# A two-layer decoder trunk on one core: the SwiGLU's second product in seven products of quarters, with two sums of weight quarters made by accumulating DMAs

## The chip, the cores and the metric

The kernel runs on one core of a Trainium2 chip. What is measured is the device time of one execution in microseconds (us). It is given as the median of several runs, and beside it stands one execution that the hardware profiler recorded, whose span is the time from the first instruction of the program to the last.

## The reference

528 tokens (16 learned meta tokens ahead of 512) of width 1024 go through two layers. Each layer is a half-step SwiGLU, a mixer (retention in layer 0, gated linear attention in layer 1) and another half-step SwiGLU, each behind an RMSNorm; a final RMSNorm follows and the meta tokens are dropped. All arrays are float32. The part that the change is about:

```python
def swiglu(x, w_in, w_out):
    gate, up = jnp.split(x @ w_in, 2, axis=-1)      # w_in [1024, 2 * 2816]
    return (jax.nn.silu(gate) * up) @ w_out          # w_out [2816, 1024]

for i in range(DEPTH):
    h = h + 0.5 * swiglu(rmsnorm(h, norm_ffn1[i]), ffn1_w_in[i], ffn1_w_out[i])
    h = h + mixer_i(rmsnorm(h, norm_mix[i]))
    h = h + 0.5 * swiglu(rmsnorm(h, norm_ffn2[i]), ffn2_w_in[i], ffn2_w_out[i])
```

## The kernel before

**Layout.** Activations lie with features on the 128 partitions and tokens along the free dimension: the residual stream is eight tiles of 128x528, the hidden layer of a SwiGLU 22 tiles. A weight chunk of 128x1024 holds, side by side, eight blocks of 128x128.

**Precision.** Every float32 operand is split into a high part (a cast, on ScalarE) and a low part (what is left, on VectorE). A product of 128x128 by 128 x tokens is three matmuls: high by high, high by low, low by high (`mm3`, lines 295 to 298). Each piece of 512 weight columns so costs one cast (`whi`, L119, ACT) and one subtraction (`wlo`, L120, DVE). DVE is VectorE, ACT ScalarE, PE TensorE, POOL GpSimd, SP SyncE.

**Weights.** The class `Weights` holds the whole plan of the weights in their order of use. It loads chunks on SP's queue into four buffers (`_load`, L88), makes pieces up to `AHEAD` = 4 ahead of the product that uses them (`fetch`, called by `hook` after each block of matmuls) and keeps seven pieces.

**Seven products of quarters.** A *unit* (`unit`) makes two tiles of a product by Winograd's form of Strassen's scheme. The weights of two tiles form a 2x2 matrix of quarters a11, a12, a21, a22 (each 128x512: half of a chunk, four blocks of 128x128), the activations one of b11 to b22 (four row tiles by half of the tokens). Seven products of quarters do the work of eight. A quarter takes 4 x 3 = 12 matmuls, a unit 84. The four sums of weight quarters s1 = a21 + a22, s2 = s1 - a11, s3 = a11 - a21 and s4 = a12 - s2 are made on DVE (`_piece`, L105); those of the activations, t1 to t4, once per sublayer (`t_sums`). A unit uses three single banks of PSUM, X, Y and Z; sums of them are taken out by DVE and ACT between the quarters, `with urgent()`, which puts these instructions ahead of others that are ready.

**A SwiGLU (`ffn`).** There are four: f1 and f2 of layers 0 and 1. The 22 hidden tiles come in six groups. The first group's four tiles are made by plain products (48 matmuls for each tile of gates and each of what they gate), while the norm, the sums t and the split of the normed input are made. The other 18 tiles are made in nine pairs, a unit for the gates (`g`) and one for what they gate (`u`). The second product of a group (`out_steps`) is plain: eight steps, one for each row tile d of the result, with (tiles of the group) x 2 halves of the tokens x 3 matmuls. These steps stand between the quarters of the next group's units; the last group's follow by themselves and feed the next sublayer (`feed`), which needs scaled and squared copies of each finished row tile. Matmuls are 264 columns wide; in the last SwiGLU, which drops the meta tokens, 256.

**Retention** uses the same units for 14 of its products; gated linear attention uses none. The row sums of the norms go through `pow` on POOL (L341, L414). In the kernel before, that is all that POOL does.

**Order.** Engines take their instructions in order. A scheduler lays this order out from the program's order and its priorities when the program is built, and may so place an instruction that is ready ahead of one that is not.

Of the kernel before, what the change touches and what calls it, by code (L numbers as in the profile page):

```python
# [16 lines left out]
P = 128  # L17
HP = P // 2
D = 1024
KD = D // P  # L20
NM = 16
# rows kept for the meta tokens
# [11 lines left out]
# keys by partitions: tiles, keys in each, and where a tile has its scores, of the queries from its own on  # L34
# [3 lines left out]
# tokens by partitions: first token, tokens in a tile, tiles; then the same of the tile that is left;  # L38
# and how many of their tokens are not in another tile
# [11 lines left out]
class Weights:  # L51
    """Streams weight chunks from DRAM and splits them, in pieces of 512 columns, into two float32r parts."""

    # the pieces of a unit: quarters of two chunks a1, a2 of 128 rows of the product, and their sums
    UNIT = ("a11", "s2", "s1", "s3", "a12", "s4", "a22")
    FIRST = ("s2", "s1", "a11", "s3", "a12", "s4", "a22")

    def __init__(self, tc, ctx, raw_bufs=4, bufs=7):
        self.nc = tc.nc
        self.raw_pool = ctx.enter_context(tc.tile_pool(name="wraw", bufs=raw_bufs))  # L60
        self.pool = ctx.enter_context(tc.tile_pool(name="wsplit", bufs=bufs))
        self.raw_bufs, self.bufs = raw_bufs, bufs
        self.chunks, self.raw = [], {}
        self.plan, self.parts, self.sums = [], {}, {}
        self.loaded = self.done = self.split = self.taken = 0
        self.live = set()
        self.sum_pool = None

    def add(self, key, ap):
        n = ap.shape[1]  # L70
        c = len(self.chunks)
        self.chunks.append(ap)
        for o in range(0, n, PW):
            self.plan.append((key, c, o, min(PW, n - o), o + PW >= n))

    def add_unit(self, key, ap1, ap2, order, between=lambda: None):
        c = len(self.chunks)
        self.chunks += [ap1, ap2]
        for q in order:
            if q == "s3":  # L80
                between()
            self.plan.append((key + (q,), c, q, PW, {"s4": c, "a22": c + 1}.get(q)))

    def _load(self):
        while self.loaded < min(self.done + self.raw_bufs, len(self.chunks)):
            ap = self.chunks[self.loaded]
            t = self.raw_pool.tile([P, CW], F32, tag="raw", name=f"raw{self.loaded}")
            self.nc.sync.dma_start(t[:, :ap.shape[1]], ap)  # L88
            self.raw[self.loaded] = t
            self.loaded += 1  # L90

    def _piece(self, c, q):
        """The column range q of a chunk, or a quarter or a sum of quarters of a pair of chunks."""
        V = self.nc.vector
        if not isinstance(q, str):
            return self.raw[c][:, q:q + PW]
        if q[0] == "a":
            o = (int(q[2]) - 1) * PW
            return self.raw[c + int(q[1]) - 1][:, o:o + PW]
        if (c, q) not in self.sums:  # L100
            a, b, op = {"s1": ("a21", "a22", V.tensor_add), "s2": ("s1", "a11", V.tensor_sub),
                        "s3": ("a11", "a21", V.tensor_sub), "s4": ("a12", "s2", V.tensor_sub)}[q]
            a, b = self._piece(c, a), self._piece(c, b)
            t = self.sum_pool.tile([P, PW], F32, tag="wsum", name=f"w{q}_{c}")
            op(t, a, b)  # L105
            self.sums[c, q] = t
        return self.sums[c, q]

    def _split(self, upto):
        oldest = min(self.live, default=self.taken)  # L110
        upto = min(upto, len(self.plan), oldest + self.bufs)
        while self.split < upto:
            i = self.split
            _, c, q, n, last = self.plan[i]
# [8 lines left out]
            if last not in (None, False):  # L123
                self.raw.pop(c if last is True else last)
                self.done += 1
                self._load()

    def prime(self, n=None):
        bufs = self.raw_bufs
        self.raw_bufs = n or bufs  # L130
        self._load()
        self.raw_bufs = bufs

    def get(self, key):
        """The pieces of a chunk, or a piece of a unit, that come next."""
# [24 lines left out]
def trunk(ctx, tc, a):  # L160
# [10 lines left out]
    # ---------------- plan of the weight chunks, in the order of use  # L171
    def plan_ffn(w_in, w_out, layer, which):
        def out(gi, ds):
            f0, f1 = GROUPS[gi]
            for d in ds:
                W.add((which, layer, "o", gi, d), w_out[layer, d, :, f0 * P:f1 * P])

        for gi, (f0, f1) in enumerate(GROUPS):
            if gi == 0:
                for f in range(f0, f1):  # L180
                    W.add((which, layer, "g", f), w_in[layer, f])
                    W.add((which, layer, "u", f), w_in[layer, NF + f])
                continue
            ds = list(range(KD))
            per = KD // (f1 - f0)
            for f in range(f0, f1, 2):
                for s, o in (("g", 0), ("u", NF)):
                    mine, ds = ds[:per], ds[per:]
                    W.add_unit((which, layer, s, f), w_in[layer, o + f], w_in[layer, o + f + 1],
                               W.FIRST if gi == 1 and f == f0 and s == "g" else W.UNIT,  # L190
                               lambda: out(gi - 1, mine[:per // 2]))
                    out(gi - 1, mine[per // 2:])
        out(len(GROUPS) - 1, range(KD))
# [5 lines left out]
    def plan_ret():  # L199
        for h in range(RH):  # L200
# [6 lines left out]
            for s, o in (("rv", 16), ("rg", 32)):  # L207
                for m in range(0, 4, 2):
                    c = o + 4 * h + m
                    if h == 0 and s == "rv":  # L210
                        W.add((s, h, m), a["ret_in"][c])
                        W.add((s, h, m + 1), a["ret_in"][c + 1])
                    else:
                        W.add_unit((s, h, m), a["ret_in"][c], a["ret_in"][c + 1],
                                   W.FIRST if h == 0 and m == 0 else W.UNIT)
# [28 lines left out]
    plan_ffn(a["f2_in"], a["f2_out"], 1, "f2")  # L244

    # ---------------- constants and the residual stream
# [17 lines left out]
    V.memset(half_neg, -0.5)  # L264

# [17 lines left out]
    def hook():  # L283
        """Between blocks of matmuls: what waits for its place in TensorE's order."""
# [15 lines left out]
    # Of PSUM, half is pairs of banks; the other half is single banks in a SwiGLU, elsewhere a pair and two banks.  # L300
# [16 lines left out]
    def proj(ps_out, w, off, nk, xh, xl, rng):  # L317
        """ps_out[m, t] = sum over nk row tiles of w's 128 columns times x."""
# [116 lines left out]
    def pair(t, halves):  # L435
        """[128, tokens] as the halves, which are equal"""
# [5 lines left out]
    def t_sums(pool, name, th, tl, halves, k, u1, u2):  # L442
# [4 lines left out]
        n = u1.shape[1]  # L447
        t = pool.tile([P, 4, n, 264], F32, tag="su", name=f"tt{name}{k}")[:, :, :, :wd]
        V.tensor_sub(t[:, 0], u1[:, :, b0:b1], u1[:, :, a0:a1])
        V.tensor_sub(t[:, 1], u2[:, :, b0:b1], t[:, 0])  # L450
        V.tensor_sub(t[:, 2], u2[:, :, b0:b1], u1[:, :, b0:b1])
        V.tensor_sub(t[:, 3], u2[:, :, a0:a1], t[:, 1])
        hi, lo = [o[k // 2][:, :, k % 2:k % 2 + n, :wd] for o in (th, tl)]
        for j in range(0, 4, 4 // n):
            c = slice(j, j + 4 // n)
            split(hi[:, c], lo[:, c], t[:, c])

    def unit(key, name, first, halves, th, tl, pool, mid, done):
# [1045 lines left out]
```

## Time and profile before

| | |
|---|---|
| median of three runs | 2157.18 us (2157.05 to 2157.83) |
| profiled execution: span | 2155.8 us |
| mean granted TensorE clock | 0.999 |
| SwiGLU f1 of layer 0: first matmul at | 6.24 us |
| retention: first matmul at | 372.11 us |
| SwiGLU f2 of layer 0 | 810.51 us |
| SwiGLU f1 of layer 1 | 1172.16 us |
| gated linear attention | 1533.81 us |
| SwiGLU f2 of layer 1 | 1794.27 us |

For the profiled execution the profiler gives the span alone; the median of the runs, which holds what lies around the span too, is 1.4 us longer. In the profile's lists a group of instructions stands as line, engine, operation, output <- inputs, shape and count; after the bar its busy time, the mean duration of one in ns, and the idle time of its engine just ahead of it with what ended it. Buffer numbers are left out, so `po_f` is the PSUM tile of the second product in all four SwiGLUs.

### The profile page before, as it was taken

To read this page: it belongs to the slowest core of one execution; us is meant where nothing else is said; L and a number is where in the kernel's file an instruction comes from. 1 tells how busy PE (TensorE), PEld (TensorE's weight loads), DVE (VectorE), ACT (ScalarE), POOL (GpSimd) and SP (SyncE) were. 2 spreads that over 40 slices of the span, in tenths; PEclk is the share of its full clock that TensorE was granted. 3 is DMA by queue.
4 is the path that set the end of the run, shared out by engine and by line. 5 is a ranking of instruction groups with operands and counts; after the bars stand their busy time and mean duration, and the time that the engine had idled before them with its cause. 6 is when DMAs were issued, how large, how long until landed. Compare 5 with 4: busy or idle time off the path is not lost.

```text
span 2155.8 us, 42829 instructions
## 1 busy us (share of the span) xinstructions
PE 2138.7 (99%) x17454; PEld 2121.4 (98%) x17454; DVE 1699.6 (79%) x3105; ACT 990.6 (46%) x1843; POOL 20.8 (1%) x25
## 2 busy tenths in 40 slices
PE   8999999999999999999999999999999999999998
PEld 8999999999999999999999999999999999999998
DVE  7887787977676788798787878787775659798886
ACT  5454445444444454454444444444633234454444
POOL 0000000000000000000000000000000000000000
PEclk9999999999999999999999999999999999999999
DMA  4333334232323222333333233333321122333332
GB/s 147 99 107 95 104 99 131 71 99 79 99 79 99 79 79 60 98 104 103 99 94 113 70 96 102 108 99 100 107 70 59 60 77 71 94 103 99 108 99 79
DMA packets 71844, 201.28 MB, mean 93 GB/s; under 512 B 8032, under 2 KB 13536, under 8 KB 71648
## 3 DMA queue, kind: packets, MB, share of 16 engines
q1 hardware_dynamic: 70640, 195.26, 29.8%
q10 hardware_dynamic: 1008, 3.29, 0.5%
q8 instruction: 137, 2.24, 0.4%
q14 instruction: 59, 0.48, 0.1%
HBM read 196.42 MB, written 2.10 MB: 92 GB/s over the span
## 4 chain that ended last, share of the span: by engine, by line
PE 97%; DVE 2%; ACT 1%; issue 0%; POOL 0%; DMA 0%; POOLq 0%; DVEq 0%; ACTq 0%
PE po_f L296 8%; PE po_f L297 8%; PE po_f L298 8%; PE po_r L298 1%; PE po_r L296 1%; PE po_r L297 1%; PE lv L1147 1%; PE po L296 1%; PE gv L296 1%; PE pk L296 1%; PE pk L297 1%; PE gv L298 1%; PE gv L297 1%; PE pk L298 1%; PE gg L296 1%; PE gg L298 1%
## 5 line engine op out<-in xcount | busy, mean ns | idle before, releaser
L119 ACT CAST whi<-raw 128x512 fp32r<-128x512 f32 (+1 forms) x653 | 397.2, 610 | 595.7 <-PE gv L297 50.0
L120 DVE TENSOR_TENSOR wlo<-raw,whi 128x512 fp32r<-128x512 f32 (+1 forms) x653 | 437.7, 673 | 94.4 <-ACT whi L119 89.5
L297 PE MATMUL po_f<-hlf,whi 128*128 128x264 f32 (+1 forms) x1344 | 380.8, 283 | 0.0
L296 PE MATMUL po_f<-hhf,whi 128*128 128x264 f32 (+1 forms) x1344 | 380.8, 283 | 0.0
L298 PE MATMUL po_f<-hhf,wlo 128*128 128x264 f32 (+1 forms) x1344 | 380.3, 283 | 0.0
L119 ACT CAST whi<-ws 128x512 fp32r<-128x512 f32 x344 | 213.1, 621 | 341.3 <-PE po_f L297 91.7
L120 DVE TENSOR_TENSOR wlo<-ws,whi 128x512 fp32r<-128x512 f32 x344 | 235.4, 685 | 23.5 <-ACT whi L119 21.4
L298 PEld LDWEIGHTS po_f<-hhf,wlo 128*128 128x128 f32 x1344 | 253.0, 188 | 0.0
L296 PEld LDWEIGHTS po_f<-hhf,whi 128*128 128x128 f32 x1344 | 253.0, 188 | 0.0
L297 PEld LDWEIGHTS po_f<-hlf,whi 128*128 128x128 f32 x1344 | 252.7, 188 | 0.0
L670 DVE SCALAR_TENSOR_TENSOR xa<-po_f,xa 128x528 f32<-128x528 f32 (+1 forms) x184 | 129.1, 701 | 109.4 <-PE po_f L298 108.7
L105 DVE TENSOR_TENSOR ws<-raw 128x512 f32<-128x512 f32 x86 | 59.3, 689 | 36.3 <-DMA raw<-in_f_in 36.2
L298 PE MATMUL po_r<-ogh,wlo 128*128 128x264 f32 x256 | 73.0, 285 | 0.0
L296 PE MATMUL po_r<-ogh,whi 128*128 128x264 f32 x256 | 72.9, 285 | 0.0
L297 PE MATMUL po_r<-ogl,whi 128*128 128x264 f32 x256 | 72.6, 284 | 0.0
L324 ACT CAST hhf<-uf 128x528 fp32r<-128x528 f32 (+1 forms) x88 | 55.3, 628 | 31.8 <-DVE uf L624 21.4
L325 DVE TENSOR_TENSOR hlf<-uf,hhf 128x528 fp32r<-128x528 f32 (+1 forms) x88 | 61.4, 699 | 3.9 <-ACT hhf L324 1.4
L105 DVE TENSOR_TENSOR ws<-ws,raw 128x512 f32<-128x512 f32 x86 | 59.0, 686 | 0.8
L105 DVE TENSOR_TENSOR ws<-raw,ws 128x512 f32<-128x512 f32 x86 | 58.8, 683 | 0.4
L105 DVE TENSOR_TENSOR ws<-raw,raw 128x512 f32<-128x512 f32 x86 | 58.7, 683 | 0.1
L296 PEld LDWEIGHTS po_r<-ogh,whi 128*128 128x128 f32 x256 | 48.3, 189 | 0.0
L297 PEld LDWEIGHTS po_r<-ogl,whi 128*128 128x128 f32 x256 | 48.3, 189 | 0.0
(647 smaller groups left out, 7065.0 us busy)
## 6 DMA issues: line engine op xcount, KB each, us to landing
raw<-in_f_in SPq DMA_DIRECT2D x176, 512.0 KB, 3.5
raw<-in_f_out SPq DMA_DIRECT2D x160, 256.0 KB, 2.7
raw<-in_ret_in SPq DMA_DIRECT2D x48, 512.0 KB, 3.5
raw<-in_gla_in SPq DMA_DIRECT2D x25, 512.0 KB, 3.5
raw<-in_ret_o SPq DMA_DIRECT2D x16, 512.0 KB, 3.5
raw<-in_f_out SPq DMA_DIRECT2D x32, 128.0 KB, 2.2
raw<-in_gla_o SPq DMA_DIRECT2D x8, 512.0 KB, 3.4
xa<-in_xT SPq DMA_DIRECT2D x8, 264.0 KB, 5.1
```

What stands on the lines that cost most here:

```text
L105: op(t, a, b)
L119: self.nc.scalar.copy(hi[:, :n], raw[:, :n])
L120: self.nc.vector.tensor_sub(lo[:, :n], raw[:, :n], hi[:, :n].bitcast(F32))
L296: nc.tensor.matmul(ps, lhsT=lh, rhs=rh, start=start, stop=False, **kw)
L297: nc.tensor.matmul(ps, lhsT=lh, rhs=rl, start=False, stop=False, **kw)
L298: nc.tensor.matmul(ps, lhsT=ll, rhs=rh, start=False, stop=stop, **kw)
L324: S.copy(hi, src)
L325: V.tensor_sub(lo, src, hi.bitcast(F32))
L670: ins = V.scalar_tensor_tensor(xv, ps[d][:, :, :wd], scale, xv, ALU.mult, ALU.add)
L1147: nc.tensor.matmul(ps[:, j, J * P:J * P + n], lhsT=Kt[:, j, J * P:(J + 1) * P], rhs=q, start=(J == 0), stop=(J == 3), skip_group_check=True)
```

## The change

The second product is made in units too. Two row tiles d, d + 1 of the result and a group of hidden tiles form the 2x2 matrix of weights, so the groups are now of eight, eight and six tiles (in the last SwiGLU six, six, six, and the last four tiles stay plain). With eight tiles a quarter has four blocks, with six three blocks (384 columns, 9 matmuls). A hidden pair of tiles is now kept as seven blocks of activations, high and low: its own three quarters and the four sums t (`hidden`, which calls `t_sums`). The first four tiles of the hidden layer stay plain products and join the first group.

A group's four units of the second product stand between the first `g` unit and the first `u` unit of the next group; the last group's come right behind its last `u` unit.

The signs move from the weights to the activations (n11, n21, n22 and n3 are negated) and to the taking out, so that the four sums become additions: s1 = a21 + a22, s3 = a21 + a11, s2 = s1 + a11, s4 = a12 + s2. Of the four sums of weights, s1 and s3 are made in a buffer `pair`, into which two plain loads on SP put a11 and a22, and a DMA from POOL's queue then adds a21 to both; s2 and s4 stay on DVE. Each unit, those of retention too, so loads the chunk a1 (`raw`), two quarters and an accumulating one into `pair`, and a quarter a22 (`half`). `pair` and `half` have two buffers each, `raw` three, pieces six.

In `unit`, the single bank X takes four of the seven products one after another, and a pair of banks QZ the other three; X is copied or read by ACT or DVE between them. The order of the pieces is now a11, s1, s2, a12, s3, s4, a22; in the first unit of a SwiGLU s1, s2, a11, a12, s3, s4, a22.

```diff
-GROUPS = ((0, 4), (4, 6), (6, 10), (10, 14), (14, 18), (18, 22))
+GROUPS = ((0, 8), (8, 16), (16, 22))
+LAST_GROUPS = ((0, 6), (6, 12), (12, 18), (18, 22))
+NPL = 4
...
-    UNIT = ("a11", "s2", "s1", "s3", "a12", "s4", "a22")
+    UNIT = ("a11", "s1", "s2", "a12", "s3", "s4", "a22")
+    FIRST = ("s1", "s2", "a11", "a12", "s3", "s4", "a22")
+    SUMS = {"s2": ("s1", "a11"), "s4": ("a12", "s2")}
...
+        n = self.width[c] = ap1.shape[1] // 2
+        self.loads["raw"].append((c, (ap1,)))
+        self.loads["pair"].append((c, (ap1[:, :n], ap2[:, n:], ap2[:, :n])))
+        self.loads["half"].append((c, (ap2[:, n:],)))
         for q in order:
+            self.plan.append((key + (q,), c, q, n, {"s3": ["pair"], "s4": ["raw"], "a22": ["half"]}.get(q, [])))
...
+                if kind == "pair":
+                    t = self.pair_pool.tile([P, 2, PW], F32, tag="pair", name=f"pair{c}")[:, :, :n]
+                    for i in range(2):
+                        nc.sync.dma_start(t[:, i], aps[i])
+                    nc.gpsimd.dma_start(t, aps[2].unsqueeze(1).broadcast_to([P, 2, n]), accum_op=ALU.add)
...
+    WITH = {"a11": ("n11", "X"), "s1": ("t1", "Z"), "s2": ("t2", "X"), "a12": ("n21", "Q"), "s3": ("n3", "X"),
+            "s4": ("n22", "Z"), "a22": ("t4", "X")}
...
+                if q == "s1":
+                    S.copy(su[:, 2], to["Z"])
+                elif q == "a11":
+                    S.copy(su[:, int(first)], X)
+                    if first:
+                        V.tensor_sub(su[:, 0], su[:, 1], su[:, 3])
+                elif q == "s2":
+                    S.copy(su[:, 3 if first else 1], X)
+                elif q == "s3":
+                    c22(X, su[:, 2])
+                elif q == "s4":
+                    row1(su[:, :2], QZ)
+                elif q == "a22":
+                    c21(X)
...
+            def hidden(f, y):
+                ...
+                    h = hp.tile([P, 2, 7, 264], F32R, tag="H", name=f"h{me}{f}")
+                    hi, lo = h[:, 0, :, :wd], h[:, 1, :, :wd]
+                    split(hi[:, 4], lo[:, 4], y[:, 0, a0:a1])
+                    t_sums(up_, f"{me}h{f}", halves, y[:, 0], y[:, 1], h[:, 0, :4], h[:, 1, :4])
+                    split(hi[:, 5:], lo[:, 5:], pair(y[:, 1], halves))
...
+            def unit_o(gi, d):
+                hs = H[gi]
+                ...
+                def row1(ab, qz):
+                    o = pair(x[d], halves)
+                    V.scalar_tensor_tensor(o, ab, -0.5, o, ALU.mult, ALU.add)
+                    ins = V.scalar_tensor_tensor(o, qz, -0.5, o, ALU.mult, ALU.add)
+                    if feed and gi == len(groups) - 1:
+                        feed(d, ins)
+
+                def c22(c, s):
+                    o = x[d + 1][:, b0:b1]
+                    V.scalar_tensor_tensor(o, s, 0.5, o, ALU.mult, ALU.add)
+                    V.scalar_tensor_tensor(o, c, 0.5, o, ALU.mult, ALU.add)
+
+                def c21(c):
+                    o = x[d + 1][:, a0:a1]
+                    ins = V.scalar_tensor_tensor(o, c, 0.5, o, ALU.mult, ALU.add)
+                    if feed and gi == len(groups) - 1:
+                        feed(d + 1, ins)
```

More of the change, by code (lines that the diff above doesn't have):

```diff
@@ new lines, in _piece @@
+        n = self.width[c]
+        if q in ("a11", "a12"):
+            o = n if q == "a12" else 0
+            return self.tiles["raw", c][:, o:o + n]
+        if q == "a22":
+            return self.tiles["half", c][:, :n]
+        if q in ("s1", "s3"):
+            return self.tiles["pair", c][:, int(q == "s1")]
+        if (c, q) not in self.sums:
+            a, b = [self._piece(c, i) for i in self.SUMS[q]]
+            t = self.sum_pool.tile([P, PW], F32, tag="wsum", name=f"w{q}_{c}")[:, :n]
+            self.nc.vector.tensor_add(t, a, b)
@@ L113, in _split @@
             i = self.split
-            _, c, q, n, last = self.plan[i]
+            _, c, q, n, over = self.plan[i]
             self._load()
@@ L122, in _split @@
             self.split += 1
-            if last not in (None, False):
-                self.raw.pop(c if last is True else last)
-                self.done += 1
+            for kind in over:
+                del self.tiles[kind, c]
+                self.over[kind] += 1
                 self._load()
     def prime(self, n=None):
-        bufs = self.raw_bufs
-        self.raw_bufs = n or bufs
+        room = self.room
+        if n:
+            self.room = {"raw": n, "half": 0, "pair": 0}
         self._load()
-        self.raw_bufs = bufs
+        self.room = room
     def get(self, key):
@@ L169, in trunk, with ffn_steps @@
     W = Weights(tc, ctx)
[L172 to L193, printed above, removed]
+    def ffn_steps(last):
+        steps = [("p", s, f) for f in range(NPL) for s in "gu"]
+        outs = []
+        groups = LAST_GROUPS if last else GROUPS
+        for gi, (f0, f1) in enumerate(groups):
+            for f in range(max(f0, NPL), f1, 2):
+                steps.append(("i", "g", f))
+                steps += outs
+                outs = []
+                steps.append(("i", "u", f))
+            plain = last and gi == len(groups) - 1
+            outs = [("l" if plain else "o", gi, d) for d in range(0, KD, 1 if plain else 2)]
+        return steps + outs
```

452 lines of the change are left out of this document (235 added, 217 removed).

## The prediction

> **What bounds the kernel now.** I read the page first, for the busy shares and the chain that ended last; then what TensorE waited for; then stretches of steady work.
>
> ```profile
> span 2155.8 us, 42829 instructions
> ...
> PE 2138.7 (99%) x17454; PEld 2121.4 (98%) x17454; DVE 1699.6 (79%) x3105; ACT 990.6 (46%) x1843; POOL 20.8 (1%) x25
> ...
> PE 97%; DVE 2%; ACT 1%; issue 0%; POOL 0%; DMA 0%; POOLq 0%; DVEq 0%; ACTq 0%
> ```
>
> ```profile
> PE pf10g L296 <- ACT whi L119: 6.2, 1, 6.2
> PE sc L296 <- DVE pl L325: 1.3, 4, 0.3
> ...
> PE bc_ro L349 <- DVE dg_ro L343: 0.7, 3, 0.3
> ```
>
> PE is busy all through, the chain is PE's own order for 97%, and its waits come to some 10 us in all, 6.2 of them the start. So matmuls taken out shorten the span one for one, as long as nothing else becomes late; and each new wait of PE costs its length. DVE, busy for 79%, is next.
>
> ```profile
> 950.00:1122.00 172.00, 172.00 (x1415) 172.00 (x1415) 140.58 (x255) 80.11 (x152) 0.00 (x0) 1.00 0.34 100
> 1860.00:2100.00 240.00, 240.00 (x2034) 240.00 (x2033) 199.97 (x366) 113.68 (x220) 0.00 (x0) 1.00 0.34 103
> 811.00:860.00 49.00, 49.00 (x399) 48.45 (x398) 42.72 (x69) 22.51 (x37) 1.53 (x2) 1.00 0.21 63
> ```
>
> These are stretches of two SwiGLUs (columns: length, then PE, PEld, DVE, ACT, POOL, then clock, DMA share and GB/s). One matmul of 264 columns takes 172.00 / 1415 = 0.1216 us, one of 256 columns 240.00 / 2034 = 0.1180. In the third, a SwiGLU's start with its plain products, DVE is busy for 87%.
>
> **What is removed.** The second product has 22 x 8 x 2 x 3 = 1056 matmuls in a SwiGLU; four times that, less the 192 of the last four tiles (`pl`), is 4032, and the page agrees (three groups of 1344):
>
> ```profile
> L297 PE MATMUL po_f<-hlf,whi 128*128 128x264 f32 (+1 forms) x1344 | 380.8, 283 | 0.0
> ```
>
> In units it is 11 pairs x 4 units x 7 x 3 = 924, so 132 fewer in three SwiGLUs; in the last, 18 tiles go from 864 to 756, 108 fewer. 396 x 0.1216 + 108 x 0.1180 = **60.9 us** less PE work. Units of the hidden layer and of retention keep their 84 matmuls.
>
> **What DVE gets.** Its costs by shape:
>
> ```profile
> L120 DVE TENSOR_TENSOR wlo<-raw,whi 128x512 fp32r<-128x512 f32 x621 | 424.4, 686 | 93.8 <-ACT whi L119 89.0
> L670 DVE SCALAR_TENSOR_TENSOR xa<-po_f,xa 128x528 f32<-128x528 f32 x144 | 101.5, 705 | 86.1 <-PE po_f L298 85.6
> L105 DVE TENSOR_TENSOR ws<-ws,raw 128x512 f32<-128x512 f32 x86 | 59.0, 686 | 0.8
> L624 DVE TENSOR_TENSOR uf<-uf,gf 128x264 f32<-128x264 f32 x81 | 34.0, 426 | 0.0
> L325 DVE TENSOR_TENSOR tlf<-ttf,thf 128x1056 fp32r<-128x1056 f32 x12 | 14.8, 1250 | 0.0
> L369 DVE SCALAR_TENSOR_TENSOR ula<-xa,gains,uha 128x528 fp32r<-128x528 f32 x40 | 30.3, 766 | 8.9 <-ACT uha L367 8.8
> L377 DVE TENSOR_TENSOR sqa_n<-sqa_n,sq_n 128x528 f32<-128x528 f32 x35 | 24.5, 701 | 0.1
> ```
>
> and two rows of its order of time:
>
> ```profile
> 2119.01 0.69 DVE L120 TENSOR_TENSOR wlo<-raw,whi 128x512 fp32r<-128x512 f32 x1
> ...
> 2119.61 0.42 DVE L624 TENSOR_TENSOR uf<-uf,gf 128x256 f32<-128x256 f32 x1
> ```
>
> They show that an instruction listed with 0.69 us lets the next start after 0.60; so sums of durations are an upper bound of DVE's time, and 0.60 / 0.69 = 0.87 of them a lower one. A hidden pair (units g and u, 168 matmuls, 20.4 us of PE) costs DVE after the change: 14 low parts and 4 sums of weights, 18 x 0.686 = 12.3; taking out, 3 of 528 and 4 of 264 columns, 3 x 0.70 + 4 x 0.43 = 3.8; `hidden`, 5 x 0.43 + 1.25 + 0.70 = 4.1. Together 20.2 us, by the lower bound 17.6. Before, four more sums (2.7) and more taking out stood against a `hidden` of 1.4. A unit of the second product (10.2 us of PE) costs 9 x 0.686 + 2 x 0.705 + 3 x 0.43 = 8.9 (lower 7.7); a plain step of four tiles cost 0.686 + 0.705 for 2.9 us of PE. A group of eight tiles, four pairs and four units, so loads DVE with 100 to 117 us per 122.5 us of PE, against 140.58 of 172 before. DVE stays below PE; I take no loss here, with a price in the first rival. At the start of a SwiGLU, `hidden` adds 2 x (4.1 - 1.4) = 5.4 to 42.72 of 49 us: full, not over.
>
> **Where PE will newly wait.** First, behind the last `u` unit. Before, steps of the group ahead stood there:
>
> ```profile
> 2119.57 0.28 PE L298 MATMUL Yf21u<-thf,wlo 128*128 128x256 f32 x1
> 2119.69 0.28 PE L296 MATMUL po_f<-hhf,whi 128*128 128x256 f32 x1
> ...
> 2122.51 0.28 PE L296 MATMUL pl<-hhf,whi 128*128 128x256 f32 x1
> ```
>
> That is 2.8 us of cover. Afterwards the last group's units follow at once and need the pair just made: c21 0.43, the sums t up to 4 x 0.43, a cast of 1056 columns about 1.1, its low part 1.25, so 3.2 to 4.5 us, over which PE has the products of the other two pairs, some 2 us. I take 2 us for each of the four SwiGLUs, **8 us** (ends 0 and 18).
>
> Second, bank X. In all orders but FIRST one quarter of another bank (1.46 us; 1.09 with three blocks) stands between two uses of X. What taking out needs:
>
> ```profile
> 510.87 0.29 PE L298 MATMUL Xrv<-uha,wlo 128*128 128x264 f32 x1
> ...
> 511.64 0.37 ACT L486 COPY surv<-Xrv 128x264 f32<-128x264 f32 x1
> ...
> 512.33 0.29 PE L298 MATMUL Yrv<-rth,wlo 128*128 128x264 f32 x1
> ...
> 512.73 0.43 DVE L490 TENSOR_TENSOR surv<-Yrv,surv 128x264 f32<-128x264 f32 x1 [0.27 <-PE Yrv L298]
> ```
>
> From the start of the last matmul ACT is done after 1.14 us and DVE after 0.83, so 1.0 and 0.7 past the time at which the next matmul could begin: below 1.46, and just below 1.09. In FIRST, a11 follows s2 in X with nothing between: 1.0 us in four SwiGLUs, **4 us** (0 to 4). For late turns in the 24 units of three blocks I take **3 us** (0 to 24, at 1 us each).
>
> Third, the last group with its feed: a unit of three blocks (63 x 0.1216 = 7.7 us of PE) costs DVE 9 x 0.55 (between 0.686 and the 0.43 of 264 columns) + 2.7 + two low parts and two sums of squares, 2 x (0.77 + 0.70): 10.6, lower 9.2. Four of them fall 6 to 12 us behind; pieces made ahead (2.4 us) and squares put off (4 x 1.4 = 5.6) cover the lower end. **3 us** for three SwiGLUs (ends 0 and 35).
>
> **The accumulating DMAs.** No row shows one. The nearest:
>
> ```profile
> raw<-in_f_in SPq DMA_DIRECT2D x176, 512.0 KB, 3.5
> raw<-in_f_out SPq DMA_DIRECT2D x160, 256.0 KB, 2.7
> ...
> q1 hardware_dynamic: 70640, 195.26, 29.8%
> ```
>
> ```profile
> L414 POOL TENSOR_TENSOR rc<-ms_n,half_neg 128x4 f32<-128x4 f32 (+2 forms) x11 | 9.1, 844 | 1177.1 <-DVE ms_n L412 1177.1
> ```
>
> 256 KB more take 0.8 us. The 512 KB of sums cost at least 3.5 us; if each byte costs like three plain ones (read, read, write), 2.7 + 5 x 0.8 = 6.7. I take the middle, 5.1. With 2.7 to 3.5 for the two loads ahead, which POOL has to wait for, the chain is 6 to 10 us. Its cover: a buffer's reload starts once s3 of its unit is split, and s1 of the unit after next is needed 10.5 pieces later, 10.5 x 1.46 = 15.3 us, 11.5 with three blocks. So it is hidden, at **0**. What hides it is PE's own work; each us beyond would cost half a us per unit (two buffers), 134 units. Traffic rises from 100 GB/s at a share of 0.34 to 1.84 MB per 10.2 us = 180 GB/s, a share of about 0.6, or 0.8 if the second read counts; landings get longer, but the engines are not full. The Trainium skill (Collectives: The Full Stack, "The bandwidth ceiling: the fold count and why AG ≠ RS ≠ AR") says that an add inside the DMA engine costs no time of its own but needs two source reads on one ring, half the rate of a copy. By that rule the sum is the 5.1 taken above; no row here can show it.
>
> On POOL, `pow` (0.84 us) queues behind a DMA that waits for its loads, and PE's broadcast of the norm for `pow`: at most 3.5 us at each of the norms that fall among units, five of them; the loads are long there by then in most, so 0 (up to 17). SP issues four loads for a unit in place of two, in the order in which buffers come free. I cost them at nothing: the transfers have the same 15 us.
>
> **Sum.** 2155.8 - 60.9 + 8 + 4 + 3 + 3 = 2112.9 us of span; with the 1.4 us by which the median stands above the span, **2114 us**.
>
> **Rivals.** *DVE becomes the bound.* If its instructions cost their full durations, the last groups cost 35 us in place of 3: 2146. For it: 20.2 us per 20.4 of PE leaves nothing to catch up with. Against: the rows above start after 0.60. *Turns of X are late all through.* Three turns in 134 units at 0.1 us are 40 us: 2154, no change. For it: DVE is fuller, and takes its order as laid out. Against: today's rows, 0.6 us to spare. *The sums land late, and the kernel is slower.* The place is ACT's cast of s1, behind which its copies out of X queue. It decides from a chain of 15.3 us, and eats the whole gain at 15.3 + 43 / 67 = 15.9; at 17 us it costs 1.7 x 67 = 114: 2228. For it: twice the traffic, POOL's descriptors and queue, none of it in the trace. Against: it needs an accumulation of 12 us, over three times a plain load. The Trainium skill (SBUF — State Buffer, "Who interferes with whom") says that a DVE instruction in a two-port mode keeps POOL from writing descriptors, while one with two SBUF inputs only blocks POOL's reads. By the first each accumulation could start later by one DVE instruction, 0.7 us, and stay inside the cover; no row here can show which holds. That the change doesn't do what it says can't be as to the matmuls, which are counted.
>
> **How the numbers follow.** Forecast 0.64 (2096 to 2134), DVE 0.14, turns 0.08, late sums 0.14. A measurement of this kernel tells 0.2% (4.3 us) from no change. The first counts as faster; DVE is split 0.07, 0.04, 0.03 and turns 0.05, 0.02, 0.01 (faster, same, slower); late sums are slower. That is 0.76, 0.06, 0.18. The range is 2096, all waits at nothing, to 2160, past the first two rivals.
>
> **What would show it.** Right: `po_f` units gone from plain steps, PE near 16950 instructions, its idle time under 35 us and at the ends of SwiGLUs; DVE at 85% or more. DVE's bound shows as waits of PE for `wlo`, the turns as waits of X's matmuls for c22 or copies, late sums as ACT's `whi` waiting for a DMA into `pair`. Wrong would be steady waits in mid-SwiGLU.

## The result and the profile after

The changed kernel takes **2473.14 us** (median; 2470.57 to 2474.71), against 2157.14 us (2157.05 to 2157.83) for the kernel before on the same chip: a ratio of 1.146, with a 95% interval of 1.145 to 1.148. Forecast were 2114 us and a range to 2160. It is slower by 316 us, and 359 us away from the forecast.

The page of the changed kernel, its span, busy time and DMA queues:

```profile
span 2468.4 us, 43589 instructions
...
PE 2208.8 (89%) x16950; PEld 2164.6 (88%) x16950; DVE 1746.6 (71%) x3183; ACT 1154.2 (47%) x2220; POOL 184.8 (7%) x159
...
q1 hardware_dynamic: 96560, 228.83, 29.2%
q0 software_dynamic: 36448, 67.12, 17.2%
```

The matmuls went as counted: 17454 - 16950 = 504. But PE now stands idle for 2468.4 - 2208.8 = 259.6 us, where it was 17.1, and its busy time has grown by 70.1 us although 60.9 us of work are gone. So 242.5 us are waits and 131 us (70.1 + 60.9) are matmuls at a slower pace. The records of the granted clock bear this out: it was 0.50 for 272 us, and half of that is 136 us. No engine is full, and DVE's share fell to 71%, which points to latency rather than throughput.

What PE waited for (total, times, longest):

```profile
PE Xf11o L339 <- DVE xa L698: 27.6, 7, 8.7
PE Xf10o L339 <- DVE xa L698: 26.6, 7, 7.4
PE Xf20o L339 <- DVE xa L698: 24.9, 7, 7.1
PE Xf21u L339 <- DVE yf L672: 20.3, 6, 4.6
...
PE Xf11g L339 <- ACT suf11g L525: 13.2, 4, 3.6
```

Every one of these is a matmul into bank X that waits for the quarter before to be taken out, in the middle of all SwiGLUs. That names the place, not the cause: the taking out costs 0.4 us, not 7. What DVE waited for, and then its group of sums s2 in the list by line:

```profile
DVE ws L134 <- DMA pair<-in_f_in: 137.0, 39, 5.9
DVE ws L134 <- DMA pair<-in_f_out: 100.7, 26, 6.7
DVE ws L134 <- issue: 37.8, 12, 5.8
```

```profile
L134 DVE TENSOR_TENSOR ws<-pair,raw 128x512 f32<-128x512 f32 (+1 forms) x134 | 89.3, 666 | 295.6 <-DMA pair<-in_f_in 137.0 <-DMA pair<-in_f_out 100.7 <-issue 37.8
```

DVE stood still for 295.6 us ahead of the 134 sums s2 = s1 + a11, the first reader on DVE of what the accumulating DMA writes. One such wait, in order of time (start, duration, engine, instruction; in brackets the idle time ahead and what ended it):

```profile
972.62 1.66 SPq L111 DMA_DIRECT2D pair<-in_f_in  x2
978.17 1.21 POOL L112 DMA_DIRECT2D pair<-in_f_in  x1 [11.29 <-DVE wlo L149]
979.43 0.43 DVE L672 TENSOR_TENSOR yf<-Xf20u,suf20u 128x264 f32<-128x264 f32 x1 [0.18 <-PE Xf20u L341]
984.39 0.69 DVE L134 TENSOR_TENSOR ws<-pair,raw 128x512 f32<-128x512 f32 x1 [4.52 <-DMA pair<-in_f_in]
986.56 0.68 DVE L149 TENSOR_TENSOR wlo<-pair,whi 128x512 fp32r<-128x512 f32 x1
987.16 0.70 DVE L667 TENSOR_TENSOR yf<-yf,gf 128x528 f32<-128x528 f32 x1
987.89 0.41 ACT L367 CAST hf<-yf 128x264 fp32r<-128x264 f32 x1 [5.03 <-DVE yf L667]
988.73 0.37 ACT L525 COPY suf20g<-Xf20g 128x264 f32<-128x264 f32 x1
989.15 0.59 PE L339 MATMUL Xf20g<-thf,whi 128*128 128x264 f32 x1 [3.92 <-ACT suf20g L525]
```

Read it from below. PE waits for ACT's copy out of X; that copy is queued behind ACT's cast of `hf`, which waits for DVE's `yf`; that is queued on DVE behind the sum s2, and s2 for the DMA. And s2 belongs to the unit that comes next: at 986.56, two microseconds later, DVE makes the low part of s3 of the unit *before* it. The scheduler has put the sum ahead of that low part, and it is the end of that low part that frees the buffer for the unit after. So DVE both asks too early and frees too late.

The DMA itself, by issues (KB each, microseconds to landing), and what issuing it costs POOL:

```profile
pair<-in_f_in SPq DMA_DIRECT2D x144, 256.0 KB, 3.9
pair<-in_f_in POOLq DMA_DIRECT2D x72, 512.0 KB, 6.2
```

```profile
L112 POOL DMA_DIRECT2D pair<-in_f_in x72 | 87.5, 1217 | 987.9 <-DMA pair<-in_f_in 355.5 <-DVE wlo L149 286.3 <-DVE hf L368 53.6
```

In the example the buffer is free at 972.6, the two loads have landed at 977.5, POOL starts at 978.17 and the sum is there at 984.3: a chain of 11.7 us. DVE had nothing else to do from 979.86 on, so the cover was 7.3 us. Over the 118 units that follow one another within 30 us, I took from the trace, for each, the time from the low part of s3 that frees the buffer to the end of the instruction ahead of s2 on DVE (the cover), and to the landing (the chain). The medians are **8.6 us of cover and 11.2 us of chain** (the middle eight tenths: 6.6 to 12.2 and 9.7 to 12.4); the sum is late in 90 of the 118, by 287 us together. In 84 of 133 pairs of neighbouring units, s2 of the later one stands ahead of the low part of s3 of the earlier one. 77 of these are among the 118: there the cover is 7.5 us, and 72 are late, by 259 us. In the other 41 the cover is 11.4 us, and 18 are late, by 29 us.

The slower pace, in three stretches around that wait (length, PE, PEld, DVE, ACT, POOL, then granted clock, DMA share, GB/s):

```profile
979.00:989.10 10.10, 6.23 (x52) 6.02 (x50) 5.39 (x12) 3.06 (x7) 0.38 (x1) 0.92 0.53 109
989.10:994.20 5.10, 5.05 (x23) 5.05 (x24) 5.02 (x9) 3.20 (x7) 1.20 (x1) 0.50 0.47 146
994.20:1000.00 5.80, 5.80 (x49) 5.80 (x49) 4.24 (x7) 3.53 (x7) 0.00 (x0) 0.99 0.71 120
```

Behind the wait the granted clock is 0.50 for 5.1 us: 23 matmuls, where 5.10 / 0.1216 = 42 fit. The wait of 3.92 us so costs 19 x 0.1216 = 2.3 us more than its length. The Trainium skill (TensorE: Matmul & The Clock Gate, Part 1: The HAM clock gate) says that after an idle window of about 3.4 us the array runs at half its clock until it has been busy for as long; the trace agrees, with 0.50 behind 3.92 us. But here a wait need not be as long as that. In retention, a wait of 1.76 us and, from 1.18 us behind its end, half the clock for 3.41 us:

```profile
841.20:842.96 1.76, 0.00 (x1) 0.00 (x1) 1.09 (x3) 0.53 (x1) 0.00 (x0) 1.00 0.04 6
844.14:847.55 3.41, 3.41 (x18) 3.41 (x17) 1.96 (x3) 0.90 (x2) 0.00 (x0) 0.50 0.74 231
```

Of the idle times of PE over 0.15 us in this trace, half the clock falls within, or begins within 3.4 us behind, all 25 of 3.5 us or more, 26 of the 37 between 1.5 and 3.5 us, and 1 of the 50 shorter ones.

### The profile page after: what moved, and what is told of

It is laid out like the page before. It is cut to its first block, busy times and chain, and to the rows that moved or that the text cites. A ratio compares the mean times of both kernels' runs of the same rounds, so it can differ in the third digit from the quotient of the medians.

```text
span 2468.4 us, 43589 instructions
## 1 busy us (share of the span) xinstructions
PE 2208.8 (89%) x16950; PEld 2164.6 (88%) x16950; DVE 1746.6 (71%) x3183; ACT 1154.2 (47%) x2220; POOL 184.8 (7%) x159
## 5 line engine op out<-in xcount | busy, mean ns | idle before, releaser
L148 ACT CAST whi<-raw 128x512 fp32r<-128x512 f32 (+1 forms) x479 | 290.5, 610 | 398.2 <-issue 33.2
L149 DVE TENSOR_TENSOR wlo<-raw,whi 128x512 fp32r<-128x512 f32 (+1 forms) x479 | 319.7, 672 | 96.9 <-ACT whi L148 96.0
L148 ACT CAST whi<-ws 128x512 fp32r<-128x512 f32 (+1 forms) x268 | 160.8, 600 | 373.7 <-PE Xf11o L340 40.5
L134 DVE TENSOR_TENSOR ws<-pair,raw 128x512 f32<-128x512 f32 (+1 forms) x134 | 89.3, 666 | 295.6 <-DMA pair<-in_f_in 137.0
L148 ACT CAST whi<-pair 128x512 fp32r<-128x512 f32 (+1 forms) x268 | 161.3, 602 | 161.2 <-PE po_r L340 13.8
L149 DVE TENSOR_TENSOR wlo<-ws,whi 128x512 fp32r<-128x512 f32 (+1 forms) x268 | 177.9, 664 | 59.9 <-ACT whi L148 57.3
L149 DVE TENSOR_TENSOR wlo<-pair,whi 128x512 fp32r<-128x512 f32 (+1 forms) x268 | 177.2, 661 | 37.3 <-ACT whi L148 37.1
L112 POOL DMA_DIRECT2D pair<-in_f_in x72 | 87.5, 1217 | 987.9 <-DMA pair<-in_f_in 355.5
L149 DVE TENSOR_TENSOR wlo<-half,whi 128x512 fp32r<-128x512 f32 (+1 forms) x134 | 88.7, 662 | 20.0 <-ACT whi L148 19.6
L134 DVE TENSOR_TENSOR ws<-raw,ws 128x512 f32<-128x512 f32 (+1 forms) x134 | 89.0, 664 | 2.6
L339 PE MATMUL Xf20o<-hf,whi 128*128 128x264 f32 x176 | 54.9, 312 | 26.0 <-DVE xa L698 24.9
```

Source lines behind the costliest of these rows:

```text
L112: nc.gpsimd.dma_start(t, aps[2].unsqueeze(1).broadcast_to([P, 2, n]), accum_op=ALU.add)
L134: self.nc.vector.tensor_add(t, a, b)
L148: self.nc.scalar.copy(hi[:, :n], raw[:, :n])
L149: self.nc.vector.tensor_sub(lo[:, :n], raw[:, :n], hi[:, :n].bitcast(F32))
L339: nc.tensor.matmul(ps, lhsT=lh, rhs=rh, start=start, stop=False, **kw)
```

## The experiments

Three theories stood at first. **A**: the sums arrive late, because DVE's order and two `pair` buffers leave them less than the chain takes. **B**: the second product in units costs more than it saves, whatever the sums are made by. **C**: the traffic and POOL's issuing hold everything up. The first four runs each change one of these.

**The sums on DVE.** The changed kernel with its units, but s1 and s3 made on DVE from one plain load of a2, and four buffers for sums in place of two.

```diff
-    SUMS = {"s2": ("s1", "a11"), "s4": ("a12", "s2")}
+    SUMS = {"s1": ("a21", "a22"), "s3": ("a11", "a21"), "s2": ("s1", "a11"), "s4": ("a12", "s2")}
...
-        self.loads["pair"].append((c, (ap1[:, :n], ap2[:, n:], ap2[:, :n])))
-        self.loads["half"].append((c, (ap2[:, n:],)))
+        self.loads["pair"].append((c, (ap2,)))
```

> The second product in seven products as changed, but s1 and s3 made by DVE from a plainly loaded chunk, no accumulating DMA. If the late sums are the cause (theory A: DVE stands at a sum s2 that waits for the accumulating DMA, and all behind it is late): no wait of DVE for a DMA into pair, TensorE idle below 40 us, clock 0.99 or more, 2100 to 2150 us, although DVE gets 268 more sums (161 to 184 us). If the second product in units is itself the cause (theory B: DVE too full, turns of bank X): above 2300 us, and the same waits of X's matmuls.

Measured: 2161.51 us, ratio 1.002 (1.001 to 1.003). The 312 us are gone, and the units are still there: B falls as the main cause. But the 504 matmuls saved bring nothing either, and this is above the 2100 to 2150 us that A gave; PE is idle for 2155.2 - 2108.4 = 46.8 us of the span, where A had less than 40. The page of this run:

```profile
PE 2108.4 (98%) x16950; PEld 2070.2 (96%) x16950; DVE 1869.7 (87%) x3451; ACT 1147.5 (53%) x2220; POOL 21.4 (1%) x25
```

**Three pair buffers.** Nothing else changed, but that `half` has one buffer, for the room.

```diff
-    def __init__(self, tc, ctx, raw_bufs=3, half_bufs=2, pair_bufs=2, bufs=6):
+    def __init__(self, tc, ctx, raw_bufs=3, half_bufs=1, pair_bufs=3, bufs=6):
```

> The change with three buffers for pair in place of two, and one for half in place of two to make room; the same DMAs and the same traffic. Theory A: the reload of a pair starts one unit (10.2 us) earlier against its use, so some 20 us of lead stand against the chain of 11.2 us: DVE's waits for pair fall from 255 us to below 30, 2100 to 2150 us. If the traffic itself is the cause (theory C: 16 DMA engines too full, so everything lands late): the waits stay, above 2300 us. If B: above 2300 us too.

Measured: 2155.61 us, ratio 0.9985 (0.9975 to 0.9994). The same transfers (302.01 MB), now at 140 in place of 122 GB/s. DVE's waits in this run:

```profile
DVE ws L134 <- DMA pair<-in_f_in: 11.2, 6, 3.0
```

11.2 us in place of 275.5 (137.0 + 100.7 + 37.8). Neither the rate of the DMAs nor POOL is the limit, and C falls; the time is 6 us above the range that A gave. DVE's order still has s2 ahead in 87 of 133 pairs; the third buffer covers it, the cover being 17.5 us in the median.

**One plain load in place of the sums.** `pair` is filled by a single load of a21, twice; the additions of a11 and a22 in s3 and s1 are left out. It shows what the kernel would take if the sums cost a load.

```diff
-                    for i in range(2):
-                        nc.sync.dma_start(t[:, i], aps[i])
-                    nc.gpsimd.dma_start(t, aps[2].unsqueeze(1).broadcast_to([P, 2, n]), accum_op=ALU.add)
+                    nc.sync.dma_start(t, aps[2].unsqueeze(1).broadcast_to([P, 2, n]))
```

> The change with one plain load of a21 on SP's queue into both halves of pair, in place of two loads and an accumulating DMA; the additions of a22 and a11 are left out. The chain from a free buffer to landed data falls from 11.2 to some 4 us, with two buffers as before. Theory A: 2100 to 2150 us. Theory B: above 2300 us.

Measured: 2144.98 us, one run, beside 2157.87 for the kernel before. So, by this one run, with the sums' chain at a load's length the change is worth 13 us, not the 43 that were forecast: a second error, which is not in the lateness of the sums (below).

**The accumulating DMAs alone.** The kernel before, second product plain as it was, with the accumulating DMAs in its 86 units. s3 is a11 + a21 there, where that kernel computes a11 - a21.

```diff
+        self.loads["raw"].append((c, (ap1,)))
+        self.loads["pair"].append((c, (ap1[:, :n], ap2[:, n:], ap2[:, :n])))
+        self.loads["half"].append((c, (ap2[:, n:],)))
         for q in order:
```

> The kernel before with s1 and s3 of its 86 units made by accumulating DMAs as in the change, the second product plain (s3 is a11 + a21 there in place of a11 - a21). Theory A: with the plain steps between, a unit of the SwiGLU lasts 16 us, more than the chain of 11.2, so only the 14 units of retention, back to back at 10.2 us, and those of the first group wait: 2155 to 2200 us. Theory C, or a fixed cost per accumulation: 86 of 134 of the 377 us that the change lost, some 2400 us.

Measured: 2170.95 us, ratio 1.0064 (1.0049 to 1.0079). In the units of the SwiGLUs nothing is lost. Plain steps of the second product stand between their quarters, so a unit takes longer and two buffers are enough. (The order of the pieces there differs too, a11, s2, s1, s3, ..., so a buffer comes free one piece earlier in a unit; no run parts the two.) In retention, where units follow one another, 8 of the 13 us are lost, the rest at the start of the first SwiGLU, and DVE's waits for the sums are back in small:

```profile
DVE ws L132 <- DMA pair<-in_ret_in: 10.8, 3, 3.9
```

Whether the accumulating DMAs do harm then depends on what lies around them; the change took those plain steps away.

After this A stood, but two things make it up, DVE's order and the number of buffers. The second four runs part them.

**The order alone.** Two buffers as in the change; only the sum s2 is put behind the low part of s1 of its own unit on DVE.

```diff
-            self.nc.vector.tensor_add(t, a, b)
+            if q == "s2":
+                with self.tc.issue_after(self.low.ins):
+                    self.nc.vector.tensor_add(t, a, b)
+            else:
+                self.nc.vector.tensor_add(t, a, b)
...
-            self.nc.vector.tensor_sub(lo[:, :n], raw[:, :n], hi[:, :n].bitcast(F32))
+            self.low = self.nc.vector.tensor_sub(lo[:, :n], raw[:, :n], hi[:, :n].bitcast(F32))
```

> The changed kernel with its two pair buffers; only DVE's order differs: the sum s2 of a unit is put behind the low part of that unit's s1, so that it no longer stands ahead of the low part of the unit before's s3, whose end frees a pair buffer. Theory A (DVE's order takes the cover: it leaves about one unit, 10 to 11.5 us, to a chain of 11.2 us): with the order as written the lead is again near the 15 us of 10.5 pieces, DVE's waits for pair fall from 275 us (137.0 + 100.7 + 37.8) to below 40, and the time to 2145 to 2175. Theory D (two buffers are too few in any order, since each is held from the first cast of s1 to the low part of s3): waits stay above 150 us and the time above 2300.

Measured: 2173.22 us, ratio 1.0068 (1.0053 to 1.0083): with two buffers **300 of the 316 us are DVE's order**, and D falls. (A third buffer alone took away 318: the order and the number of buffers cause the loss together, and mending either one removes nearly all of it.) The timeline at the same place:

```profile
958.60 0.81 SPq L112 DMA_DIRECT2D pair<-in_f_in  x2
963.77 1.21 POOL L113 DMA_DIRECT2D pair<-in_f_in  x1 [8.95 <-DMA pair<-in_f_in]
967.99 0.69 DVE L154 TENSOR_TENSOR wlo<-pair,whi 128x512 fp32r<-128x512 f32 x1
974.88 0.68 DVE L154 TENSOR_TENSOR wlo<-pair,whi 128x512 fp32r<-128x512 f32 x1
975.48 0.68 DVE L137 TENSOR_TENSOR ws<-pair,raw 128x512 f32<-128x512 f32 x1
```

The low part of s3 (967.99) now comes first, frees the other buffer, and the sum s2 stands behind the low part of its s1 (974.88, 975.48); its data had landed at 969.7. No wait of DVE for `pair` is left. The chain is as long as before (median 11.4 us); the cover of s2 is 16.3 us in the median, and that of ACT's cast of s1, now the first reader, 14.0. A stretch of the second SwiGLU shows what the change was meant to give:

```profile
900.00:1060.00 160.00, 160.00 (x1315) 160.00 (x1314) 136.71 (x240) 94.07 (x187) 19.36 (x16) 1.00 0.70 180
```

PE is full at clock 1.00, DVE at 85%, with 180 GB/s at a DMA share of 0.70. What is left of A is in the last SwiGLU, where the units of the second product have three blocks. ACT's waits, PE's, and the worst of the five:

```profile
ACT whi L153 <- DMA pair<-in_f_in: 19.1, 5, 5.9
...
PE Xf21o L344 <- ACT suf21o L534: 16.1, 5, 5.4
```

```profile
1885.01 0.86 SPq L112 DMA_DIRECT2D pair<-in_f_in  x2
1891.91 1.20 POOL L113 DMA_DIRECT2D pair<-in_f_in  x1 [8.23 <-DVE wlo L154]
1900.68 0.62 ACT L153 CAST whi<-pair 128x512 fp32r<-128x512 f32 x1 [5.32 <-DMA pair<-in_f_in]
1901.21 0.36 ACT L534 COPY suf21o<-Xf21o 128x256 f32<-128x256 f32 x1
```

Here the loads took 6.2 us and the sum 8.6, a chain of 15.5 us from 1885.0 to 1900.5, while ACT was ready at 1895.4. The cast of s1 waits, and the copy out of X behind it. This is to the letter the rival of the prediction, only in 5 turns and not in 134 units.

**The order and three pair buffers.**

> The same order and three pair buffers (one buffer of the lone quarters in place of two). Theory A: with the order put right the third buffer has nothing left to cover; within 6 us of the kernel with the order alone, and at or below the 2155.6 of three buffers in the old order, since the sum s2 no longer holds up the copies out of PSUM behind it on DVE: 2143 to 2156. Theory D: the third buffer brings over 100 us against the order alone.

Measured: 2148.46 us, ratio 0.9948 (0.9931 to 0.9964), so 25 us below the order alone. I had expected 6 at most; the three-block units were the difference, for the 23.6 us between the spans of the two profiles all lie in the last SwiGLU. Against three buffers in the old order it gains 7 us.

**Plain ends.** The order, and in every SwiGLU groups of 6, 6, 6 and 4 tiles, with the last one's products as they stand.

```diff
-        groups = LAST_GROUPS if last else GROUPS
+        groups = LAST_GROUPS
...
-            plain = last and gi == len(groups) - 1
+            plain = gi == len(groups) - 1
```

> The order put right, and every SwiGLU ends as the last one does: groups of 6, 6, 6 and 4 tiles, the last group's products as they stand instead of by units. That adds 24 matmuls in each of three SwiGLUs, 72 by 0.1216 = 8.8 us. If the ends of the SwiGLUs cost the 6 to 7 us each that stand in the trace with plain loads in place of the sums, these 19 us go and the kernel is about 10 us faster than with the order alone (2135 to 2160). If that time only moves (DVE behind at the ends whatever the products are), it is 5 to 10 us slower.

Measured: 2249.97 us, ratio 1.0425 (1.0409 to 1.0441), 77 us above the order alone; neither expectation held. Its waits:

```profile
PE Xf11o L344 <- ACT suf11o L534: 17.9, 4, 7.0
PE Xf21o L344 <- ACT suf21o L534: 16.4, 6, 5.9
PE Xf10o L344 <- ACT suf10o L534: 15.0, 3, 5.6
PE Xf20o L344 <- ACT suf20o L534: 13.3, 4, 5.4
PE po_f L344 <- ACT hf L372: 11.8, 3, 4.3
```

Four of the rows are the turns of three-block units, now in all four SwiGLUs: it confirms that two buffers don't cover these. The fifth is what the run was for: the plain end waits up to 4.3 us for the last hidden pair, so plain products don't take that wait away.

**s1 and s3 in buffers of their own**, in the old order; s1's comes free behind s2.

```diff
-        self.loads["pair"].append((c, (ap1[:, :n], ap2[:, n:], ap2[:, :n])))
+        self.loads["p1"].append((c, (ap2[:, n:], ap2[:, :n])))
+        self.loads["p3"].append((c, (ap1[:, :n], ap2[:, :n])))
```

> The order of the changed kernel, but s1 and s3 in buffers of their own, two of each, each with a plain load and an accumulating DMA of 256 KB, so POOL issues twice as many. s1's buffer comes free behind the sum s2 and not behind the low part of s3. Theory A: the chain of s1 then starts about one unit (10 us) earlier than it is needed now, and no wait is left but that of s3, behind which less hangs: 2145 to 2180. Theory E (the rate of the accumulating DMAs or POOL's issuing is the limit, not when a buffer is free): as slow as the changed kernel or slower, 2450 to 2600.

Measured: 2161.34 us, ratio 1.0016 (1.0006 to 1.0025), with twice as many accumulating DMAs (POOL 293 instructions, 255.7 us, in place of 159 and 184.8). E falls: it is when the buffer comes free that counts.

**Where the rest went.** For these runs I added up by place what lies between the starts of neighbouring matmuls beyond 0.1216 us (0.1180 with 256 columns), where that is over 25 ns. *Starts* are the plain products of the first four tiles, *g, u* the units of the hidden layer, *out* the second product. The differences of the last column, less the 60.9 us of matmuls, agree with those of the spans to within 1.1 us.

| us | starts | g, u | out | retention | linear attention | sum |
|---|---|---|---|---|---|---|
| before | 5.7 | 0.0 | 2.1 | 21.7 | 13.2 | 42.7 |
| changed | 18.3 | 174.6 | 161.9 | 46.9 | 13.9 | 415.6 |
| order | 20.1 | 9.4 | 50.4 | 24.7 | 13.2 | 117.8 |
| order, three buffers | 18.9 | 3.4 | 34.1 | 24.8 | 13.1 | 94.2 |
| the same, low parts first (below) | 6.7 | 9.7 | 31.7 | 24.9 | 13.0 | 85.9 |

With the late sums gone, 51.5 of the 60.9 us are lost again, 32.0 in the second product and 13.2 at the starts. The last two runs take up one of these each.

**The hidden pair first.** Order and three buffers, and the work on a finished hidden pair goes ahead of low parts of weights.

```diff
-                    split(hi[:, 4], lo[:, 4], y[:, 0, a0:a1])
+                    with urgent():
+                        split(hi[:, 4], lo[:, 4], y[:, 0, a0:a1])
...
```

> Sum s2 behind the low part of s1, three pair buffers, and in addition what the hidden pair needs after its second half is final (its sums and low parts on DVE, its casts on ACT) goes ahead of low parts of weights. At the end of each of three SwiGLUs 4.3 to 4.4 us are lost at the first units of the last group, of which the traces show waits of 0.97 us for ACT's copy and 1.09 us for the low part of the hidden pair, and matmuls at half pace behind them. Theory F (the order of DVE makes that wait: two low parts of weights, 0.95 us, stand ahead of the pair's): the second wait goes and the ends lose 2 to 3 us each instead of 4.4; 2139 to 2146 in all. Theory G (what is late there is the chain of sums itself, and a low part of the weights moved back costs PE the same): no change within 3 us, 2146 to 2152.

Measured: 2151.11 us, ratio 0.997 (0.9959 to 0.9982): no gain, as G has it. But the edit changed nothing at the place: DVE's order around this low part is the same as without it at all three ends, and so are PE's two waits (0.80 and 0.93 us of idle time; 0.97 and 1.09 above are counted between the starts of matmuls). So the time doesn't decide between F and G; the rows do. Low parts of weights stand on DVE while ACT casts the pair, but its own low part comes 0.18 us behind the end of the cast (335.29), with the edit and without it:

```profile
333.57 0.43 DVE L499 SCALAR_TENSOR_TENSOR ttf10h<-yf,ttf10h 128x264 f32<-128x264 f32 x1
334.21 1.08 ACT L372 CAST hf<-ttf10h 128x1056 fp32r<-128x1056 f32 x1
335.00 0.55 DVE L154 TENSOR_TENSOR wlo<-half,whi 128x384 fp32r<-128x384 f32 x1
335.47 1.25 DVE L373 TENSOR_TENSOR hf<-ttf10h,hf 128x1056 fp32r<-128x1056 f32 x1
```

So the low parts ahead of it cost 0.2 us at most. What is late is the pair's chain of sums, cast and low part, behind which PE has only the other two pairs' products. What would shorten it wasn't tried.

**Low parts first.** Order and three buffers, and the low parts of the plain chunks' weights go ahead of the sums of the input.

```diff
+            if isinstance(q, str):
+                self.low = self.nc.vector.tensor_sub(lo[:, :n], raw[:, :n], hi[:, :n].bitcast(F32))
+            else:
+                with self.tc.high_priority(offset=HEAD_START):
+                    self.nc.vector.tensor_sub(lo[:, :n], raw[:, :n], hi[:, :n].bitcast(F32))
```

> Sum s2 behind the low part of s1, three pair buffers, and in addition the low parts of the plain chunks' weights go ahead of the input's sums in DVE's order. Waits for such low parts at the starts of the four SwiGLUs lose 6.4 us at 48 to 58 us and 1.3 to 1.9 us in the others. If DVE is full there (9.70 and 10.00 us of 10 between 30 and 50 us), the work only changes places and the first units wait for their sums instead: 2146 to 2152. If the order alone makes the wait, about 8 us go: 2137 to 2143.

Measured: **2140.83 us**, ratio 0.9924 (0.9911 to 0.9938), the fastest of all and below both kernels. The start of the first SwiGLU with the order and three buffers, behind a wait for the low part `wlo` that ended at 52.28, and with the low parts first:

```profile
48.60:52.30 3.70, 0.33 (x4) 0.12 (x2) 3.70 (x11) 1.07 (x1) 0.00 (x0) 0.91 0.00 0
52.30:58.50 6.20, 6.20 (x28) 6.20 (x29) 6.20 (x10) 1.48 (x2) 0.00 (x0) 0.50 0.35 117
```

```profile
43.00:60.00 17.00, 17.00 (x142) 17.00 (x141) 17.00 (x32) 8.98 (x15) 0.00 (x0) 1.00 0.10 32
```

DVE is full in both, and the work that now comes later does make the first units wait (g, u: 9.7 us in place of 3.4). But those are several short waits, 1.5 us at most, with half the clock once for 3.4 us (from 70.7), in place of one of 3.4 us with half the clock for 6.2 us. So the order alone made most of that wait, and I had put "only changes places" ahead of it.

## Why the prediction was wrong

- **Matmuls, -60.9 us**: right, 504 fewer, and PE full at 0.1216 us wherever nothing is late.
- **The accumulating DMAs, 0: the step that failed.** "A buffer's reload starts once s3 of its unit is split, and s1 of the unit after next is needed 10.5 pieces later, ... 15.3 us." For ACT's cast of s1 that was about right (14.0 us with the order put right). But I counted the cover to the first reader in the program's order, on one engine. DVE reads the buffer too, for s2, and its order is the scheduler's: s2 stood ahead of the low part of s3 that frees the other buffer. That left 8.6 us of cover for a chain of 11.2, and with two buffers this order makes 300 us.
- **The chain, 6 to 10 us: too short.** It is 11.2: the two loads 4.4 in place of 2.7 to 3.5, 0.7 until POOL starts, which had no term, and 6.0 in place of 5.1 for the sum. By the rule of the Trainium skill that I cited (Collectives: The Full Stack, "The bandwidth ceiling: the fold count and why AG ≠ RS ≠ AR") the sum was estimated at those same 5.1 us; the measured number decides. Against 15.3 us of cover the longer chain would have done no harm in units of four blocks.
- **Three-block units: 11.5 us of cover, at 0.** In the last SwiGLU, which has 12 of the 24 units, two buffers don't suffice even in the right order, with a chain of 15.5 us in the example: 25 us between two and three buffers.
- **The late-sums rival (0.14)** had the right mechanism, but neither its place nor its price. It named ACT's cast of s1, and said that lateness would begin with a chain of 15.3 us. The place was DVE's s2, and lateness began at some 8.6 us. ACT's cast is the place in the 5 turns above.
- **"Each new wait of PE costs its length"**: too little. With the clock at 0.50 for 5 us behind a wait of 3.9, it costs 6.2. Over the kernel that is the 131 us of slower matmuls beside 242.5 us of waits, 0.54 us for each us of waiting.
- **The ends and turns, 18 us.** 32 us in the second product with the order and three buffers, in place of 8 + 4 + 3 + 3; the mechanisms (the last hidden pair, turns of three-block units, the feed) are the ones that the trace shows, at about twice the price. At the last hidden pair, half the clock for 3.4 us is part of it, behind two waits of 0.80 and 0.93 us within 3.4 us (from 338.4).
- **The starts, 0** ("full, not over"): 13.2 us. DVE was full, and its order put the input's sums ahead of the low parts that PE waited for; 12.2 of these went with the low parts first, though 6.3 came back in the units.
- **DVE as the bound (0.14)**: not shown. Full stretches have DVE at 85% with PE at 100%. Two more sums per unit on it (the first run) cost 13 us against the order with three buffers.
- **Traffic**: 180 GB/s at a share of 0.70, between the 0.6 and 0.8 of the forecast, and no limit there. The chain of 15.5 us in the run with the order alone fell in a stretch at 216 GB/s and a share of 0.84 (1885.0 to 1900.5), so denser traffic may have lengthened it; no run shows that by itself.

## What to carry to other kernels

A transfer's cover is counted from the instruction that frees the buffer to the first instruction on *any* engine that waits for the data, in the order that the scheduler lays out, not that of the program: an instruction that waits for a DMA and is placed early on an in-order engine blocks all behind it, even what would have freed the next buffer. Before work is moved from an engine into a chain of DMAs, add up every link of the chain, the waits between queues too, and give it a buffer more or pin its first reader's place. And a wait of PE can cost more than its length: in this kernel all waits together, with the slower clock behind them, cost one and a half times theirs.

## What was not expected of the hardware

- An accumulating DMA of 512 KB took 5.9 to 7.1 us from issue to landing (medians of groups of the runs), where a plain load of 512 KB took 3.4 to 4.9; issuing it occupied POOL for 1.2 us, and it started 0.7 us behind the landing of the loads that it waited for. While 216 GB/s were moved, one chain stretched to 15.5 us.
- The granted clock fell to 0.50 not only behind waits of 3.4 us and more but also behind one of 1.76 us, and behind two of 0.80 and 0.93 us close together, in each of these for 3.41 us.
